# Segment mean on one core: the id probes are queued 26 rows ahead of the data they belong to

## The chip, the cores and the metric

The kernel runs on one core of one Trainium2 chip. The metric is device time in microseconds (us) for one execution; a profile's "span", from the first to the last instruction, is 1 to 2 us shorter than the time of the same run. Medians of three or more runs are quoted. A ratio is the mean time of one kernel's fast runs over the mean of the other's fast runs of the same rounds, so it is not quite the ratio of the medians. A run is called slow here when it is over 1.5% above the fastest of its kernel.

## The reference

Ten million values with sorted segment ids; the result is the mean of each of 10,000 segments.

```
n = 10_000_000; num_segments = 10000
data        = randn(n)  float32
segment_ids = sort(randint(0, num_segments, n))      # int64
sums[id] += data;  counts[id] += 1                   # over all n
out = sums / max(counts, 1)
```

## The kernel before

The array is laid out as 128 partitions of 78,125 values, cut along the partition into 98 rows of 800 values. A segment is about 1,000 values long, so the kernel relies on at most one segment boundary in a row (a slow general path behind a branch covers all other inputs; it is not taken here). For each row it needs three things:

- **Probes.** The id at every 160th position, five for a row. They say whether there is a boundary in the row and in which 160 values. Reading them is a strided DMA: 8 bytes out of every 1,280.
- **A gather.** The 159 ids in that stretch, read by an indirect DMA that GpSimd issues (one per row). Their sum gives the exact boundary.
- **The data.** ScalarE sums the row (`total`); VectorE sums the part in front of the boundary (`split`).

VectorE runs a fixed order of instructions. "First look" (five steps, which need the probes and end in issuing the gathers) stands 22 rows ahead of its group of rows; "second look" (which needs the gathers) stands 4 rows ahead:

```python
GROUPS = [4, 6, 8, 10, 10, 10, 10, 10, 10, 10, 10]   # rows per probe group
X_PROBE = 32                                         # how far ahead of row r things are queued
X_LOOK = 22
... dpool = tile_pool(name="dpool", bufs=18)         # 18 data tiles of two rows = 36 rows

def first_look(g):
    a, b = bounds[g], bounds[g + 1]
    ...
    def s1():                                        # the first reader of the probes
        nc.vector.tensor_tensor(out=eq, in0=in0b, in1=in1b, op=ALU.is_equal)
    ...
    def s5():
        nc.vector.scalar_tensor_tensor(out=IDX[:, a:b], ...)
        gather(g)                                    # one indirect DMA for each row

def split(r):
    nc.vector.scalar_tensor_tensor(out=junk_v[:, 0:n], in0=iota[:, 0:n], scalar=KK[:, r : r + 1],
        in1=d, op0=ALU.is_lt, op1=ALU.mult, accum_out=A[:, r : r + 1])
...
for g in range(NG):
    steps = first_look(g)
    if g < HEAD: after[-1] += steps                  # groups 0 to 2: in front of row 0
    else:
        for i, f in enumerate(steps):
            after[max(bounds[g] - X_LOOK, 0) + i].append(f)
...
CHECK_AT = 80; IF_AT = 84; C1 = 66; C2 = 95
after[CHECK_AT].append(verdict)                      # one segment boundary per row everywhere?
after[IF_AT].append(branch)                          # the general path, not taken
after[IF_AT].append(tables_a)                        # outputs of the first rows
after[C2 + 1].append(tables_b)

for r in range(-X_PROBE, NR):
    while pnext < NG and bounds[pnext] <= r + X_PROBE:
        load_probes(pnext); pnext += 1               # SP queue
        if pnext == 2: ...                           # snt, a small load, also on SP
    while nt < NT and 2 * nt <= r + X_PROBE:
        load_data(nt); nt += 1                       # SP queue, two rows in each
    if r >= 0: total(r); split(r)
    if r >= -1:
        for f in after[r]: f()
```

All probes and data go through one queue, issued by SP, in this order. The probes of the group that starts at row b stand just in front of row b's data.

## Time and profile before

| | before |
|---|---|
| time, median of 3 runs | 230.07 us (229.84 to 230.25) |
| span of the profiled run | 228.8 us |
| VectorE's waits for probes | 60.5 us, 10 waits |
| last probes read by VectorE, after row 66 | 160.2 us |
| last data load landed | 171.6 us |
| VectorE's last instruction ends | 217.7 us |

The page's slices of the kernel before: busy tenths of VectorE (DVE), ScalarE (ACT) and the DMA engines in 40 slices of 5.72 us, and what the DMA moved.

```profile
DVE  5210600933895980994992991994999898999900
ACT  2637273691682573483483493470000079400000
DMA  6999999999999999999999999999993200000000
GB/s 117 233 358 231 340 351 167 418 270 272 402 288 232 408 347 174 408 321 219 404 345 181 404 368 174 408 351 163 407 396 99 61 3 1 1 0 0 6 3 0
```

DMA is full to slice 29 (counted from 0) and then falls off, while VectorE has gaps until the DMA is nearly done and is full afterwards. The regular dips in GB/s are probes: tiny elements keep the DMA busy and move little. The waits of the kernel before (engine, line, who was waited for: us in total, times, longest):

```profile
ACT junk_a L373 <- DMA data_t<-in_data_dram: 68.4, 32, 6.1
DVE eq L305 <- DMA pr<-in_segment_ids_dram: 60.5, 10, 12.0
```

ScalarE waits for data, as a DMA bound kernel should. VectorE never waits for data at all: it waits for probes, at L305, the first instruction of the first look. The timeline shows how such a wait looks (start, duration, engine, line, operation, in brackets the idle time before it and what ended it). First VectorE at the last two waits, then SP issuing the last group's probes, which VectorE reads at 160.22 us, then where ScalarE was:

```profile
137.30 1.05 DVE L378 SCALAR_TENSOR_TENSOR junk_v<-iota,q_116,data_t 128x800 bf16<-128x800 f32 x1
138.28 0.08 DVE L378 DVE_READ_ACCUMULATOR junk_v<-iota,q_116,data_t 128x1 f32 x1
143.27 0.20 DVE L305 TENSOR_TENSOR eq<-pr 128x40 f32<-128x40 int32 x1 [4.91 <-DMA pr<-in_segment_ids_dram]
...
160.22 0.20 DVE L305 TENSOR_TENSOR eq<-pr 128x40 f32<-128x40 int32 x1 [3.31 <-DMA pr<-in_segment_ids_dram]
160.33 0.17 DVE L307 CAST q_116<-pr 128x10 f32<-128x10 int32 x1
160.41 1.04 DVE L378 SCALAR_TENSOR_TENSOR junk_v<-iota,q_116,data_t 128x800 bf16<-128x800 f32 x1
```

```profile
142.83 0.42 SPq L225 DMA_DIRECT2D pr<-in_segment_ids_dram  x1
143.36 17.45 SPq L232 DMA_DIRECT2D data_t<-in_data_dram  x5
```

```profile
153.28 0.87 ACT L373 ACTIVATE junk_a<-data_t 128x800 bf16<-128x800 f32 x1
154.06 0.19 ACT L373 ACTIVATION_READ_ACCUMULATOR junk_a<-data_t 128x1 f32 x1
```

The last group's probes are issued at 142.83 us and read at 160.22 us, 17 us later, because of what lies before them in the queue. The Trainium skill ("DMA: Bandwidth & Descriptors", Queues, rings and completion order) says that each DMA engine consumes the descriptors of one queue in ring order; the trace fits that: these 50 KB loads took a median of 17.3 us from issue to landing. Counting the `split` instructions, the one at 160.41 us is row 67; the `total` at 153.28 us is row 84, after which ScalarE is stopped by the branch. When VectorE has done row 66, ScalarE has long done row 84, and the data up to row 87 stand in front of the awaited probes in the queue.

### The profile page before, as it was taken

How to read it: one execution, taken by the hardware profiler on the slowest of the kernel's cores; microseconds unless marked ns; L12 is line 12 of the kernel's file. 1: busy time of each engine (PE TensorE's matmuls, PEld its weight loads, DVE VectorE, ACT ScalarE, POOL GpSimd, SP SyncE). 2: the span in 40 equal slices, each digit the busy share in tenths (PEclk: the TensorE clock that was granted, in tenths of full speed). 3: DMA queues.
4: the chain of work that ended last, by engine and by line, in shares of the span. 5: the costliest groups of instructions: out<-in, count | busy, mean ns of one | idle time of the engine just before them, and what ended most of it. 6: DMA issues, size and time to landing. Idle time of an engine off the chain costs nothing. (4 is left out here: it accounts for less than half of the span.)

```text
span 228.8 us, 1187 instructions
## 1 busy us (share of the span) xinstructions
PE 1.6 (1%) x6; PEld 1.4 (1%) x6; DVE 149.9 (66%) x443; ACT 95.4 (42%) x197; POOL 102.5 (45%) x113
## 2 busy tenths in 40 slices
PE   0000000000100000000000000000000000000000
PEld 0000000000100000000000000000000000000000
DVE  5210600933895980994992991994999898999900
ACT  2637273691682573483483493470000079400000
POOL 3674471077277576077377277167367300000110
DMA  6999999999999999999999999999993200000000
GB/s 117 233 358 231 340 351 167 418 270 272 402 288 232 408 347 174 408 321 219 404 345 181 404 368 174 408 351 163 407 396 99 61 3 1 1 0 0 6 3 0
DMA packets 74733, 53.39 MB, mean 233 GB/s; under 512 B 65306, under 2 KB 65389, under 8 KB 74720
## 3 DMA queue, kind: packets, MB, share of 16 engines
q1 hardware_dynamic: 69952, 40.51, 61.7%
q0 software_dynamic: 4768, 12.78, 21.1%
q14 instruction: 13, 0.11, 0.1%
HBM read 56.46 MB, written 0.04 MB: 247 GB/s over the span
## 5 line engine op out<-in xcount | busy, mean ns | idle before, releaser
L344 POOL DMA_INDIRECT GT<-in_segment_ids_dram,IDX x98 | 98.2, 1002 | 76.9 <-DVE IDX L335 28.0
L373 ACT ACTIVATE junk_a<-data_t 128x800 bf16<-128x800 f32 x98 | 85.0, 867 | 101.0 <-DMA data_t<-in_data_dram 68.4
L378 DVE SCALAR_TENSOR_TENSOR junk_v<-iota,q_116,data_t 128x800 bf16<-128x800 f32 x98 | 102.4, 1045 | 1.1
L305 DVE TENSOR_TENSOR eq<-pr 128x40 f32<-128x40 int32 (+3 forms) x11 | 2.2, 196 | 60.5 <-DMA pr<-in_segment_ids_dram 60.5
L358 DVE TENSOR_REDUCE GS<-GT 128x6 f32<-128x954 int32 (+1 forms) x17 | 18.8, 1104 | 0.2
L373 ACT ACTIVATION_READ_ACCUMULATOR junk_a<-data_t 128x1 f32 x98 | 18.3, 186 | 0.0
L584 POOL DMA_INDIRECT out_dram<-out_140,AN x1 | 1.0, 1018 | 36.3 <-DVE out_140 L555 36.3
L378 DVE DVE_READ_ACCUMULATOR junk_v<-iota,q_116,data_t 128x1 f32 x98 | 8.1, 83 | 0.0
L363 DVE TENSOR_TENSOR kr<-QQ,GS 128x6 f32<-128x6 f32 (+1 forms) x17 | 2.7, 160 | 0.0
L366 DVE TENSOR_TENSOR q_116<-kr,q_116 128x6 f32<-128x6 f32 (+1 forms) x17 | 2.7, 159 | 0.0
L314 DVE TENSOR_SCALAR ST<-jc 128x10 f32<-128x10 f32 (+3 forms) x11 | 2.2, 198 | 0.0
L239 DVE CAST iota<-i_i 128x800 f32<-128x800 int32 x1 | 1.0, 995 | 1.7 <-POOL i_i L238 1.7
L310 DVE TENSOR_REDUCE jc<-eq 128x10 f32<-128x40 f32 (+3 forms) x11 | 2.1, 187 | 0.0
L318 DVE TENSOR_SCALAR NB<-q_116 128x10 f32<-128x10 f32 (+3 forms) x11 | 2.0, 183 | 0.0
L584 POOL DMA_INDIRECT out_dram<-out_141,AN x1 | 1.0, 992 | 2.1 <-issue 2.1
L328 DVE TENSOR_TENSOR pos<-ST,wb 128x10 f32<-128x10 f32 (+3 forms) x11 | 1.8, 165 | 0.0
L307 DVE CAST q_116<-pr 128x11 f32<-128x11 int32 (+4 forms) x11 | 1.8, 166 | 0.0
L335 DVE SCALAR_TENSOR_TENSOR IDX<-NB,pos 128x10 int32<-128x10 f32 (+3 forms) x11 | 1.8, 165 | 0.0
L329 DVE SCALAR_TENSOR_TENSOR QQ<-q_116,ST 128x10 f32<-128x10 f32 (+3 forms) x11 | 1.8, 161 | 0.0
L311 DVE TENSOR_TENSOR q_116<-q_116 128x10 f32<-128x10 f32 (+3 forms) x11 | 1.7, 159 | 0.0
L373 ACT ACT_TABLE_LOAD x1 | 1.3, 1283 | 0.8 <-PEq L691 0.8
L482 PE MATMUL badp<-bad,ones 128*128 128x1 f32 x2 | 0.6, 362 | 121.6 <-DVE bad L481 121.6
(93 smaller groups left out, 28.7 us busy)
## 6 DMA issues: line engine op xcount, KB each, us to landing
data_t<-in_data_dram SPq DMA_DIRECT2D x48, 800.0 KB, 9.7
GT<-in_segment_ids_dram,IDX POOLq DMA_INDIRECT x98, 6.0
data_t<-in_data_dram SPq DMA_DIRECT2D x1, 662.5 KB
pr<-in_segment_ids_dram SPq DMA_DIRECT2D x7, 50.0 KB, 17.3
pr<-in_segment_ids_dram SPq DMA_DIRECT2D x1, 48.0 KB, 17.3
pr<-in_segment_ids_dram SPq DMA_DIRECT2D x1, 40.0 KB, 12.5
pr<-in_segment_ids_dram SPq DMA_DIRECT2D x1, 30.0 KB, 8.0
pr<-in_segment_ids_dram SPq DMA_DIRECT2D x1, 21.0 KB, 3.6
```

Source lines behind the costliest of these rows:

```text
L305: nc.vector.tensor_tensor(out=eq, in0=in0b, in1=in1b, op=ALU.is_equal)
L307: nc.vector.tensor_copy(out=V[:, a:e], in_=pr32[:, a:e, 0])
L310: nc.vector.tensor_reduce(out=jc, in_=eq, axis=AX.X, op=ALU.add)
L314: nc.vector.tensor_scalar(out=ST[:, a:b], in0=jc, scalar1=float(S), scalar2=float(1 + W), op0=ALU.mult, op1=ALU.add,)
L318: nc.vector.tensor_scalar(out=NB[:, a:b], in0=BT[:, a:b], scalar1=-1.0, scalar2=1.0, op0=ALU.mult, op1=ALU.add)
L344: nc.gpsimd.indirect_dma_start(out=GT[:, r % RING, :], out_offset=None, in_=ids2d[:], in_offset=bass.IndirectOffsetOnAxis(ap=IDX[:, r : r ...
L358: nc.vector.tensor_reduce(out=GS[:, a:b], in_=gt32[:, s : s + b - a, 0 : 2 * W : 2], axis=AX.X, op=ALU.add)
L363: nc.vector.tensor_sub(out=kr, in0=QQ[:, a:b], in1=GS[:, a:b])
L366: nc.vector.tensor_mul(out=KK[:, a:b], in0=kr, in1=BT[:, a:b])
L373: nc.scalar.activation(out=junk_a[:, 0:n], in_=d, func=ACT.Copy, accum_out=T[:, r : r + 1])
L378: nc.vector.scalar_tensor_tensor(out=junk_v[:, 0:n], in0=iota[:, 0:n], scalar=KK[:, r : r + 1], in1=d, op0=ALU.is_lt, op1=ALU.mult, accum_ ...
L584: nc.gpsimd.indirect_dma_start(out=out2d[:], out_offset=bass.IndirectOffsetOnAxis(ap=AN[:, i : i + 1], axis=0), in_=o[:], in_offset=None,)
```

## The change

The intent is to have the probes in place long before VectorE's first look comes to them, so that VectorE can work on data as they land.

```diff
-X_PROBE = 32
+X_PROBE = 26
+X_DATA = 26
 X_LOOK = 22
...
-    for r in range(-X_PROBE, NR):
-        while pnext < NG and bounds[pnext] <= r + X_PROBE:
+    for r in range(-X_PROBE - X_DATA, NR):
+        while pnext < NG and bounds[pnext] <= r + X_PROBE + X_DATA:
             load_probes(pnext)
...
-        while nt < NT and 2 * nt <= r + X_PROBE:
+        while nt < NT and 2 * nt <= r + X_DATA:
             load_data(nt)
```

Instructions and their order on VectorE, ScalarE, GpSimd and TensorE stay the same. The *lead* is the number of rows by which the probes are queued ahead of their own row's data; it was 0 and becomes 26. Only SP's order of loads differs: four probe groups (28 rows), then one data tile, then a probe group in front of every fifth tile; the last 18 tiles have no probes among them.

## The prediction

> **What bounds the kernel now.** Two stages follow each other.
>
> 1. To about 171 us, the DMA queue: the page's slices show DMA at 9 tenths from slice 2 to slice 29, at 160 to 418 GB/s. The dips are the probes, 65,306 packets under 512 B (the Trainium skill, "DMA: Bandwidth & Descriptors", Rules for kernel authors: a strided last dimension becomes one descriptor per element; the trace agrees).
> 2. From 160.4 to 217.7 us, VectorE: the timeline shows no wait above 1 us there. Then 11 us for the last scatter and the end.
>
> Why is VectorE late? The first look at the group that starts at row b stands after row b-22 in VectorE's order, but its probes are queued just ahead of row b's data, so VectorE stays 22 rows behind the data's front. The waits show it: 60.5 us for probes in 10 waits, 44 us of it after row 0. At 160.2 us the last probes land; VectorE has done row 66, while ScalarE finished row 84 at 154 us. When all data are in, some 22 rows and the tables are still to do.
>
> **What the change does.** No instruction is added or removed. The SP queue's order changes: four probe groups (28 rows) go ahead of the first data tile, each later group 26 rows ahead of its data, and the last 18 data tiles have no probes among them. X_DATA of 26 should not matter. First looks find their probes landed; VectorE waits on data instead and runs at the data's front. DMA work is the same.
>
> **Cost.** ScalarE's waits date the landings: the first tile after each probe group landed at 57.8, 75.9, 94.1, 110.6, 128.3, 145.5 us, so 17.5 us for ten rows: five tiles at an estimated 2.0 us (800 KB at the best slices' 410 GB/s), ten gathers at an estimated 0.3 us, and 4.3 us left for probes. VectorE is active 12 to 13 us for ten rows, so it keeps up.
>
> After the last probes 36 rows remain (from row 62, tile 31). Tile 39 landed at 145.5 us before; tile 31 will have eight tiles fewer (-16 us) and ten rows of probes more (+4.3) ahead of it: about 134.5 us. From row 62 VectorE needs what it needs now: 57.3 us (rows 67 to 97, verdict, tables) plus 7 us for five rows and a second look. Data with gathers then arrive at 1.0 to 1.3 us a row, VectorE's 1.3, so it should hardly wait. VectorE ends at 134.5 + 64.3 = 199 us; with 11.1 us of end the span is 210, the time 211.5. The start (row 0 near 20 us instead of 27) is not on the path. SP's small snt load (5.9 to 8.9 us) may leave the queue empty for up to 3.5 us: a risk on the slow side.
>
> Predicted: 211.5 us, 205 to 218. Chances: faster 0.95, same 0.04, slower 0.01.
>
> **What would show it right.** VectorE's wait for probes falls from 60 us to below 15, all before row 0; its waits are on data instead; the last data lands at 171 to 176 us as before; no VectorE wait over 2 us after 140 us; gathers all landed before 165 us; the stretch from verdict to end, 50 us, unchanged.
>
> **What would make it wrong.** Probes slower when alone at the start; gathers that now meet the data so that the second look waits for them; SP stalled early by the snt load; data waiting for buffers.

## The result, and the profile after

| | before | after |
|---|---|---|
| time, median of 4 runs each | 230.16 us (229.84 to 230.36) | 214.12 us (214.03 to 214.22) |
| ratio | | 0.9304, 95% interval 0.9288 to 0.9321 |
| span of the profiled run | 228.8 us | 212.4 us |
| VectorE's waits for probes | 60.5 us | 4.3 us |
| VectorE's waits for data | none | 34.5 us |
| last probes read, after row 66 | 160.2 us | 142.7 us |
| last data load landed | 171.6 us | 177.2 us |
| VectorE's last instruction ends | 217.7 us | 201.2 us |

Lines of the changed kernel have numbers higher by one. The slices (5.31 us each) and waits that answer to those above:

```profile
DVE  5425169848955984993886787589999888999800
ACT  2002047517624753762663664377876598000000
DMA  6699999999999999999999999999999990000000
GB/s 9 36 97 243 250 400 377 145 385 398 270 234 405 397 96 382 391 232 278 403 325 184 396 404 89 402 393 401 415 399 396 406 395 14 0 0 0 7 2 0
```

```profile
ACT junk_a L374 <- DMA data_t<-in_data_dram: 79.8, 41, 17.7
DVE junk_v L379 <- DMA data_t<-in_data_dram: 34.5, 21, 6.0
DVE GS L359 <- DMA GT<-in_segment_ids_dram,IDX: 5.0, 1, 5.0
DVE eq L306 <- DMA pr<-in_segment_ids_dram: 4.3, 1, 4.3
DVE sel_134 L549 <- SPq L627: 0.8, 1, 0.8
```

The dips of GB/s end at slice 24 (about 130 us): from there the queue holds data alone, at 393 to 415 GB/s beside the last gathers. The data did not come sooner: the rate falls to 8 GB/s only in the 2 us after 176 us. Before, the data were in at 171.6 us, and gathers alone, at 82 to 115 GB/s, went on to 180 us. VectorE's waits moved from `eq` to `junk_v`: from probes to data. One new line, the last, will matter below. The timeline of VectorE around the landing of row 62 (tile 31, the first tile after the last probes):

```profile
135.38 1.05 DVE L379 SCALAR_TENSOR_TENSOR junk_v<-iota,q_116,data_t 128x800 bf16<-128x800 f32 x1 [3.36 <-DMA data_t<-in_data_dram]
...
141.42 1.05 DVE L379 SCALAR_TENSOR_TENSOR junk_v<-iota,q_116,data_t 128x800 bf16<-128x800 f32 x1 [0.76 <-DMA data_t<-in_data_dram]
...
142.69 0.20 DVE L306 TENSOR_TENSOR eq<-pr 128x40 f32<-128x40 int32 x1
```

Row 62 starts at 135.38 us (predicted: about 134.5), waiting for its data. At 142.69 us the last probes are read with no wait, 17.5 us earlier than before; the span is shorter by 16.4 us, so that difference is the gain to within about a microsecond.

The chain of waits, however, does not lead back through VectorE to row 62. It starts here (start, duration, what):

```profile
177.34 0.21 DVE sel_134 L549
177.55 0.65 DVE sel_134 L555
...
178.95 1.06 DVE junk_v L379 x2
```

and the timeline says what held L549, a copy of `fbt` in the first tables, with SP's own instructions at the branch beneath it (operation, count: duration in ns, first and last start):

```profile
177.34 0.21 DVE L549 COPY sel_134<-fbt 128x48 f32<-128x48 f32 x1 [0.83 <-SPq L627]
```

```profile
L627 SPq EVENT_SEMAPHORE  x8: 17/17/17, 168.7 to 177.4; - x8
```

In the kernel before the same eight instructions took from 185.0 to 185.6 us and held nothing up:

```profile
L626 SPq EVENT_SEMAPHORE  x8: 17/17/17, 185.0 to 185.6; - x8
```

SP passes the branch and then eight semaphore instructions, of which the first five start about 2 us apart. The packed trace shows what they wait for: the semaphores of SP's last five data loads are complete at 168.70, 170.72, 173.30, 175.27 and 177.22 us, and each of the five instructions waits on one of them and starts within 0.02 us of its completion. So after the branch SP waits until its own outstanding data loads have landed. `fbt` is what the general path writes by SP, so VectorE's copy of it waits for SP. Before the change the data were long in by then (171.6 us against 185.0). Now VectorE arrives there 17 us earlier and meets the end of the data.

### The profile page after: what moved, and what is told of

Read it like the earlier page. It is cut to its first block, busy times and chain, and to the rows that moved or that the text cites. A ratio compares the mean times of both kernels' runs of the same rounds, so it can differ in the third digit from the quotient of the medians.

```text
span 212.4 us, 1195 instructions
## 1 busy us (share of the span) xinstructions
PE 1.6 (1%) x6; PEld 1.4 (1%) x6; DVE 149.7 (70%) x443; ACT 95.4 (45%) x197; POOL 102.2 (48%) x113
## 2 busy tenths in 40 slices
DMA packets 74733, 53.39 MB, mean 251 GB/s; under 512 B 65306, under 2 KB 65389, under 8 KB 74720
## 5 line engine op out<-in xcount | busy, mean ns | idle before, releaser
L379 DVE SCALAR_TENSOR_TENSOR junk_v<-iota,q_116,data_t 128x800 bf16<-128x800 f32 x98 | 102.4, 1045 | 35.4 <-DMA data_t<-in_data_dram 34.5
```

## The experiments

Every kernel gave correct results. Twelve kernels ran; each was timed beside the kernel before on the same chip. My theory throughout: VectorE's lag behind the data's front is what costs; it is the look-ahead of the first look (22 rows) less the lead. The main rivals: the gain comes from the order of DMA traffic itself, or from the smaller look-ahead of the data. The medians and ratios to the kernel before:

| run | what differs | median us | ratio (95%) |
|---|---|---|---|
| data32 | after, data 32 ahead | 214.57 | 0.9318 (0.9299 to 0.9336) |
| level26 | after, lead 0 | 230.41 | 0.9999 (0.9978 to 1.0021) |
| lead12 | after, lead 12 | 218.58 | 0.9492 (0.9477 to 0.9508) |
| lead18 | after, lead 18 | 213.96 | 0.9287 (0.9272 to 0.9303) |
| lead44 | after, lead 44 | 215.94 | 0.9388 (0.9351 to 0.9425) |
| lead98 | after, all probes first | 225.73 (3 fast runs) | 0.9773 (0.9739 to 0.9808) |
| read_early | after, first reader of the probes 26 rows earlier | 232.78 | 1.0085 (1.0035 to 1.0135) |
| look18 | before, first look 18 rows ahead | 224.87 | 0.9756 (0.9735 to 0.9776) |
| snt_first | after, snt memsets first | 212.71 | 0.9250 (0.9222 to 0.9278) |
| best18 | snt_first, lead and look 18 | 213.04 | 0.9238 (0.9215 to 0.9261) |
| best16 | snt_first, lead and look 16 | 213.78 | 0.9270 (0.9244 to 0.9295) |
| tables_late | best18, first tables after row 92 | 210.34 | 0.9146 (0.9119 to 0.9173) |

### The two halves of the edit: data32 and level26

```diff
-X_DATA = 26
+X_DATA = 32          # data32
```
```diff
-X_PROBE = 26
+X_PROBE = 0          # level26
```

> The changed kernel with the data issued 32 rows ahead as before, probes still 26 rows ahead of their data. My theory (only the probes' lead over their data matters; buffers and the queue's depth pace the data): same as the changed kernel, 214.1 us, within 0.5. Rival (the smaller data look-ahead of 26 is part of the gain): slower than 216.

> The changed kernel with a lead of 0: probes level with their data, everything issued 26 rows ahead. My theory: the time of before, 230.1 us, within 0.6, with VectorE waiting about 60 us for probes again. Rival (the look-ahead of 26 is part of the gain): clearly under 229.

Measured: 214.57 us and 230.41 us. The whole gain belongs to the lead of the probes; the data's own look-ahead does nothing.

### The place of the reader, not of the load: read_early and look18

If VectorE's lag is the cause, moving the reader must do the same as moving the load. In read_early the new queue order stays, and only the first step of the first look goes 26 rows further ahead, to 48 rows (`eq` gets 8 buffers instead of 3 so that this is free of hazards):

```diff
-            for i, f in enumerate(steps):
+            after[max(bounds[g] - X_LOOK - X_PROBE, 0)].append(steps[0])
+            for i, f in enumerate(steps[1:], 1):
                 after[max(bounds[g] - X_LOOK, 0) + i].append(f)
```

> The changed kernel, queue order untouched; only the instructions that first read a group's probes stand 26 rows earlier in VectorE's order (48 rows before the group instead of 22). My theory (what costs is that VectorE waits for probes at a place 22 rows or so ahead of the data it could work on): the wait comes back, VectorE resumes at row 41 when the last probes land near 133 us and has 57 rows left: about 237 us (232 to 240), slower than before although the DMA order is the new one. Rival (the gain comes from the DMA order itself: no probes among the last 18 data tiles, data and gathers mixed better): stays near 214.

Measured: 232.78 us, 0.9% above the kernel before, although the loads are queued in the new order. VectorE's waits for probes came back, and others with them, for which the profile names no DMA:

```profile
DVE eq L306 <- DMA pr<-in_segment_ids_dram: 37.6, 4, 16.3
DVE eq L306 <- issue: 6.4, 2, 6.0
DVE junk_v L379 <- remote: 4.2, 2, 2.6
DVE junk_v L379 <- issue: 4.0, 2, 3.1
```

The rival (DMA order alone: 214) is refuted as it stands: with the order of the loads kept, moving one step of the first look lost the whole gain. But not all of that loss is lag. The last wait for probes ended at 89.7 us, after row 20; from there waits of the other kind, which are described under lead98, add up to 14.2 us in the profiled run (234.32 us). Without them it would have taken an estimated 220 us, 6 us more than the changed kernel and not 20. My number was inside the range by luck: the last probes were already in when VectorE came to them at 124.7 us, where I had expected it to stand at row 41 until 133 us, and waits that I did not foresee made up most of the difference. The next run is the cleaner test.

look18 takes the kernel before and moves the reader the other way:

```diff
-X_LOOK = 22
+X_LOOK = 18
```

> The kernel before, queue order untouched; the first look stands 18 rows ahead of its group instead of 22. My theory: VectorE lags the data by 18 rows, four rows less at 1.3 us, minus about 1.4 us for gathers that come later: about 226.3 us (224.5 to 227.5). Rival (DMA order alone): 230.

Measured: 224.87 us, so 5.4 us from four rows of lag, with no load moved: about 1.3 us a row, VectorE's time for a row, and nothing was lost to later gathers. Its profile has none of the other waits after row 0. That the order of the loads is untouched here rules out that only their order counts.

### How much lead: lead12, lead18, lead44, lead98

```diff
-X_PROBE = 26
+X_PROBE = 12         # and 18, 44, 98
```

> The changed kernel with a lead of 12 rows. My theory (VectorE's lag is 22 rows less the lead): the last probes land seven tiles and some gathers later than with 26, near 150 us, with VectorE at row 66 and 58 us left: about 220.8 us (218.5 to 222.5). Rival (every row of lead is worth the same, 16 us over 26 rows): 222.7.

> The changed kernel with a lead of 18 rows. My theory: the last probes land near 143.8 us with VectorE at row 66; in the changed kernel VectorE reaches that place at 142.7 us; so 214 to 215.5 us, the gain saturates before a lead of 22. Rival (linear in the lead): 219.

> The changed kernel with a lead of 44 rows. Theory A (DMA and VectorE work alone decide: row 44 lands near 113.3 us, VectorE then needs 1.3 us a row and reaches row 62 at 136.7 us instead of 135.4): 215.5 us (214.5 to 216.5). Theory B (what made a lead of 98 miss by 12 us, waits of VectorE on its own results while it runs unbroken beside a full DMA queue, starts as soon as data are waiting): 217 to 222, with such waits in the profile.

> The changed kernel with all probes ahead of all data. My theory: the first data tile lands near 55 us, from there VectorE never waits and has 146 us of work left: 201 us, plus 11 us of end: about 214 us (211 to 219), so no further gain. Rival (more lead is always better, or probes alone run faster): under 209.

Measured: 218.58, 213.96, 215.94 and 225.73 us. Up to 18 rows the lead pays, and between 18 and 26 it is flat. (In lead18, as in the changed kernel and in data32, the copy of `fbt` waited for SP, so SP's limit sets all three times; but the wait is 0.8 to 0.9 us in each, so VectorE's own arrival there is the same too.) lead12 fell below the linear rival (222.7) and at the fast edge of my range: the last probes were read at 148.0 us, where I had estimated 150. The time is thus not linear in the lead, as the lag theory says.

lead44 lies in the range of theory A, but not for A's reason: VectorE there waits 2.55 us for SP at the copy of `fbt`, because the data ended later (the last load landed at 178.6 us, against 177.2), a limit that neither theory names. Its profile also holds 3.4 us of the waits of theory B, before 136 us.

lead98 missed by 12 us. The first tile landed near 50 us, even sooner than I had assumed, but VectorE then lost 16.4 us (the sum of its waits that are not for data, gathers, probes or TensorE after row 0) in waits such as these:

```profile
104.71 1.05 DVE L379 SCALAR_TENSOR_TENSOR junk_v<-iota,q,data_t 128x800 bf16<-128x800 f32 x1 [0.70 <-DVE junk_v L379]
...
106.81 1.05 DVE L379 SCALAR_TENSOR_TENSOR junk_v<-iota,q,data_t 128x800 bf16<-128x800 f32 x1 [0.73 <-DVE q L308]
...
108.91 0.17 DVE L312 TENSOR_TENSOR q<-q 128x10 f32<-128x10 f32 x1 [0.94 <-DVE jc L311]
111.71 1.05 DVE L379 SCALAR_TENSOR_TENSOR junk_v<-iota,q,data_t 128x800 bf16<-128x800 f32 x1 [2.63 <-remote]
```

The data were not missing: the instruction at 111.71 us is row 38, which ScalarE summed at 97.36 us:

```profile
97.36 0.87 ACT L374 ACTIVATE junk_a<-data_t 128x800 bf16<-128x800 f32 x1 [0.54 <-DMA data_t<-in_data_dram]
```

In the changed kernel VectorE has no wait of this kind above 0.2 us after row 0. Here the starts of the held instructions stand close to multiples of 0.70 us apart (104.71, 106.81, 108.91 and 111.71 us: 2.10, 2.10 and 2.80), in spells of about 10 us. ScalarE is held in the same spell, up to 1.12 us, with nothing shown that it waits for. read_early has such waits too, and the fast runs of lead98 and read_early differ by 2.4 and 2.9 us among themselves, those of the changed kernel by 0.2 (one of the four runs of lead98 was slow and is in neither its median nor its ratio). They are not confined to kernels in which data wait for VectorE: the profiles of data32, lead44 and snt_first hold 2.7, 3.4 and 6.9 us of them. I do not know what holds these instructions. "More lead is always better" is refuted by the two runs; why the extreme one costs so much is open.

### The start: snt_first

SP's small load of `snt` waits until 5.85 us for two memsets that stand last among VectorE's preparations, and between 6 and 7 us the DMA share is 0.02. The edit only moves the memsets to the front:

```diff
     snt32 = snt.bitcast(I32)
+    nc.vector.memset(snt32[:, 0:1], NSEG)
+    nc.vector.memset(snt32[:, 1:2], 0)
...
-    nc.vector.memset(snt32[:, 0:1], NSEG)
-    nc.vector.memset(snt32[:, 1:2], 0)
```

> The changed kernel with the two memsets of snt made first on VectorE instead of after the others, so that SP's load of snt does not wait until 5.8 us for them. My theory (the middle is bound by the DMA queue, which was empty for some 2 us near 6 to 7.5 us, and every later landing is late by that): about 212.2 us (211.5 to 213.3). Rival (the start is not on the path, as my prediction said of VectorE's start): 214.1.

Measured: 212.71 us, 1.4 us less than the median after the change. It ran on the same chip as lead18 (213.96 us, ratio 0.9287), against which it gains 1.2 us by the medians, 0.9 us by the ratios. Its last data load landed at 175.65 us, 1.6 us earlier than in the changed kernel. An empty queue at the start is on the path of a kernel bound by that queue, even when the engine that starts late is not.

### The new limit: best18, best16 and tables_late

```diff
-X_PROBE = 26
+X_PROBE = 18         # best16: 16
-X_LOOK = 22
+X_LOOK = 18          # best16: 16
```

> The early snt memsets, a lead of 18 and a first look 18 rows ahead instead of 22. My theory: the last probes (before row 70) no longer hold VectorE at row 66; it reaches row 70 when its data land, near 144 us with the early snt, where the changed kernel had row 70 at 148.0 us: about 210.0 us (208.5 to 211.7), against 212.7 of the early snt alone. Rival (nothing below a lead of 26 is left to gain, and later gathers cost): 212.7 or more.

> The same with lead and first look at 16. My theory: two rows more of VectorE at the data's front (2 us), against a second look that waits about 2 to 4 us for the last group's gathers: 209 to 212 us, no clear gain over 18. Rival (gathers cost nothing): 208.

Measured: 213.04 and 213.78 us, with no gain over snt_first and both above my ranges. My 210.0 for best18 was wrong, and its profile shows most of the reason. VectorE computed the verdict's flag at 162.50 us, 1.5 us earlier than in snt_first (164.00 us) and 3.5 us earlier than in the changed kernel (166.04 us). Then it waited for SP, 2.38 us against 1.29 and 0.83 us there, and so gave back about 1.1 us of the 1.5 and 1.6 us of the 3.5:

```profile
175.36 0.21 DVE L551 COPY sel<-fbt 128x48 f32<-128x48 f32 x1 [2.38 <-SPq L627]
```

```profile
L627 SPq EVENT_SEMAPHORE  x8: 17/17/17, 166.7 to 175.4; - x8
```

From this copy to the end of the span it is 35.0 us in best18 (175.36 to 210.4) and 35.1 us in the changed kernel (177.34 to 212.4): a fixed tail behind the landing of the data. (The profiled run of best18, 212.18 us, is the fastest of the five; the 0.9 us up to their median is not explained.) best16 lost its gain elsewhere: the second look after row 80 waited 3.38 us, at the place where I had expected the last group's gathers to be late.

If so, moving that copy past the landing must free VectorE. The last run does it by placing the first tables after row 92:

```diff
-    after[IF_AT].append(tables_a)
+    after[IF_AT + 8].append(tables_a)
```

> The kernel with early snt memsets, lead and first look 18, and now the first tables after row 92 instead of row 84; no work is added or removed. My theory: there the copy of fbt waited 2.38 us for SP, which after the branch first waits for all its data loads (to 175.4 us); after row 92 VectorE comes to it near 180 us, past that, and the wait vanishes: span 208.0 instead of 210.4 us, about 210.0 us (209.3 to 211.0). Rival (the wait belongs to the branch or VectorE merely waits elsewhere, the end is bound by the last data all the same): 212 to 213.5.

Measured: 210.34 us, 209.12 to 211.53. SP passes at the same time as ever, and the copy now comes behind it, with no wait:

```profile
L627 SPq EVENT_SEMAPHORE  x8: 17/17/17, 167.3 to 175.6; - x8
```

```profile
182.23 0.20 DVE L551 COPY sel<-fbt 128x48 f32<-128x48 f32 x1
```

It is 2.7 us below best18 by the medians and the fastest version of all, 8.5% below the kernel before; its spread of 2.4 us is wider than that of most others.

## Why the prediction was right, and where it was not

- **The cause**, VectorE's lag of about 22 rows behind the data because its first look waited for probes queued level with the data: right. Its wait for probes fell from 60.5 to 4.3 us, all in front of row 0, as predicted; look18 shows it by moving only the reader, lead12, lead18 and level26 by moving only the loads; read_early points the same way, with its size blurred by waits whose cause is open.
- **X_DATA does not matter**: right (data32, 214.57 us).
- **DMA work is the same**: right in the packets and bytes (74,733 and 53.39 MB in both). The last data load landed at 177.2 us, slightly outside the predicted 171 to 176 us and 5.6 us later than before (171.6 us).
- **The sum.** Row 62 lands at 135.38 us, predicted 134.5. From there VectorE takes 65.9 us to its last instruction, predicted 64.3; the difference is 0.83 us for SP, 0.76 us for the data of row 66, and little else. The end took 11.2 us for 11.1. Together 214.1 for 211.5 us, in the range and 2.6 us on the slow side.
- **The step that was incomplete**: "From row 62 VectorE needs what it needs now". It does, but a second limit lay one microsecond behind it, and the prediction did not have it. After the branch SP waits for its data, VectorE for SP, and 35 us of work follow. That the two limits meet within 0.83 us in the changed kernel is luck; it is why the time came out nearly right. best18, predicted with the same sum, failed by 3.0 us; in its profiled run this wait is 2.38 us.
- **"The start is not on the path"**: right of VectorE's start, wrong of SP's. The empty queue that I had listed as a risk of up to 3.5 us costs about 1.2 to 1.4 us (snt_first).
- **Gathers all landed before 165 us**: slightly missed. The last one was issued at 161.09 us; with the median of 6.1 us to landing it came near 167 us. Nothing waited for it.
- **No VectorE wait over 2 us after 140 us; the stretch from verdict to end unchanged at 50 us**: right. The longest is 0.83 us, and the stretch is 50.5 us (161.90 to 212.4) against 49.6 before (179.21 to 228.8).

## What to carry to other kernels

When an engine runs a fixed order, what decides is not only when a load is issued but where its first reader stands: a reader 22 rows ahead, fed by a load level with the data, holds the engine 22 rows behind the data, and moving either end by a row was worth about one row of that engine's work (1.0 us a row in lead12, 1.3 us in look18) until another limit came. A lead a little short of the reader's distance was already enough (18 rows for 22); all probes first cost 12 us against that, in waits whose cause is open. When a bottleneck is removed, look at what the engine will reach earlier: here it was a wait behind a branch that had been free for as long as the engine was late, and it swallowed the next improvement until its reader was moved behind it.

## What the Trainium skill lacked or had wrong

- "DMA: Bandwidth & Descriptors", Rules for kernel authors, says that a strided last dimension becomes one descriptor per element, but gives no rate for 8-byte elements. In lead98, from 34 to 46 us, when probes alone were being moved, the rate was 14 GB/s; that is an estimated 1.75 elements per ns, or 3.7 us for the 6,400 elements of ten rows, where 5 tiles of 800 KB for the same rows take an estimated 10 us at the 410 GB/s of good slices.
- The same page, Where 436 GB/s comes from, says that for HBM to SBUF the HBM side, about 358 GB/s, binds. The changed kernel moved 393 to 415 GB/s from HBM to SBUF in every slice from 25 to 32 (counted from 0), some 40 us on end, with one core in use. The page's own single-core measurement (425 GB/s at 16 MB) is nearer.
- No page that I found tells that SP, after a branch in such a program, waits for its outstanding loads (eight semaphore instructions, 168.7 to 177.4 us after the change, with the last load landing at 177.2 us; 185.0 to 185.6 us before, with the last load at 171.6 us), nor that an engine that later reads what the branch could have written waits for SP with it: 0.83 us after the change, 2.38 us in best18.
- No page that I found explains VectorE's waits of 0.3 to 3.0 us behind its own instructions, 16.4 us in all in lead98. Their cause is open.
